# A mixture-of-experts stage on one Trainium2 core: VectorE's work around the first expert pair put in another order

## The chip, the cores and the metric

The kernel runs on one core of a Trainium2 chip. The time is device time in microseconds (us) of the whole program. The run with the profiler takes one execution apart; its span goes from the first to the last instruction.

## The reference

The program is two model blocks one behind the other, on 512 tokens of 1024 values in float32. The change touches the last stage of the second block, a mixture of 32 experts in 4 groups:

```python
def hier_moe(h, router_group_w, router_expert_w, w_gate, w_up, w_down):
    ...                                   # one group per token, two experts of 8 in it
    gate = group_prob * top_p / jnp.sum(top_p, axis=-1, keepdims=True)
    expert_id = (group_idx[:, None] * EXPERTS_PER_GROUP + top_local).astype(jnp.int32)
    ...                                   # tokens sorted by expert into slots
    def expert_block(args):
        xblk, e = args
        a = xblk @ w_gate[e]
        b = xblk @ w_up[e]
        return (jax.nn.silu(a) * b) @ w_down[e]
    yb = lax.map(expert_block, (xb, block_expert)).reshape(P, D)
    out = jnp.zeros((N + 1, D), jnp.float32).at[slot_tok].add(yb.astype(jnp.float32) * slot_gate[:, None])
    return out[:N].astype(h.dtype)
```

An expert's weights are three matrices of 1024 x 512 values (gate, up and down).

## The kernel before, in words

Each expert has 56 slots for tokens; what does not fit is handled by a loop at the very end (`overflow`), for which `spill` works out the tables. Experts go in pairs (16 of them, `blks`), and four pairs, an octet, share one gather.

`route` finds for each token its two experts and their slot numbers (`dest`). `build_S` turns `dest` into one-hots `S3` for the 448 slots of an octet, with 16 operations on VectorE (lines 1663 and 1664), and up to two that shift `dest` (`db`, line 1654). `gather_T` multiplies the tokens by these one-hots: 64 matmuls, out of which VectorE and ScalarE write the gathered tokens `hT` (`mhT`). `slot_rows` lays the slot numbers (`rows`) and gates (`grow`) of all tokens along the free dimension. From them, for each pair, `slots` makes the one-hots `ST` that later bring the results back to the tokens, and `gates` sums up the gate of each slot (`us`; line 1749, four operations and a sum, line 1753).

The products of a pair: `gate_up` multiplies `hT` by gate and up weights of one expert (two halves of the weights, four transfers of 1 MB, 32 matmul instructions), and `gu_out` on ScalarE scales the result by `us` (line 1804). `act_T` transposes it on TensorE and makes `h2`: tanh on ScalarE (line 1821) and two products on VectorE (lines 1822 and 1823). `down` multiplies by the down weights. `y_out` splits the output in two parts for the sums (ScalarE line 1862, VectorE line 1863), and `combine` adds it to the tokens: 16 matmuls with `ST`, and eight additions on VectorE (line 1872).

The loop of `moe` (lines 1454 on) goes over the pairs p: the first expert's gate and up product of p, the down product of the second expert of p-1, the transposes, the second expert's product with the sums of p-1 and the slots of p between its two halves, the gather where p ends an octet, the gates of p+1, the down product of the first expert of p, the transposes of the second.

What sets the order: TensorE's instructions run in the order of the source (`self.ordered(nc.tensor)`). On the other engines a scheduler puts the instructions in an order of its own; a call of `self.after(a, b)` makes it put a behind b without a wait on the chip. Each engine then works its queue off in that order, so that a waiting instruction holds up what stands behind it. Tiles have tags with a number of buffers; the scratch of `route` and `spill` has the tags yh0 and yl0, which `y_out` uses afterwards. The tile `h2` has the tag "rt" in the pool `rp` with one buffer (line 522), "hx" in the first pair and "S3" at the very end. Weights go through 16 buffers of 1 MB, loaded from SyncE's queue in the order of use.

Of the kernel before, what the change touches and what calls it, by code (L numbers as in the profile page):

```python
# [10 lines left out]
F32 = mybir.dt.float32  # L11
# [6 lines left out]
ALU = mybir.AluOpType  # L18
# [111 lines left out]
class Model:  # L130
# [1289 lines left out]
    def moe(self, psd):  # L1420
# [9 lines left out]
        blks = []  # L1430
# [8 lines left out]
        nb = NPAIR  # L1439
# [10 lines left out]
        self.slot_rows()  # L1450
        blks[0]["first"] = True
        ov = []
        for p in range(nb):
            more = p + 1 < nb

            def sums():
                if p:
                    self.combine(blks[p - 1], [(t, n) for n in range(2) for t in range(NT)])
                self.slots(blks[p])
                if more and p % 4 == 3:  # L1460
                    self.build_S(octs[p // 4 + 1])

            self.gate_up(blks[p], 0, not p, None if more else sums)
            if not p:
                self.gates(blks[0])
                self.gu_out(blks[0], 0)
            elif more:
                self.down(blks[p - 1], 1)
                self.act_T(blks[p], 0)
                self.y_out(blks[p - 1])  # L1470
            self.gate_up(blks[p], 1, half=sums if more else lambda: self.act_T(blks[p], 0))
            if more:
                if not p:
                    self.act_T(blks[0], 0, "hx")
                if p % 4 == 3:
                    self.gather_T(octs[p // 4 + 1])
                self.gates(blks[p + 1])
                self.down(blks[p], 0)
                self.act_T(blks[p], 1, "rt" if p else "hx")
                if not p:  # L1480
                    ov.extend(self.spill(mc))
                if p + 2 == nb:
                    self.down(blks[p], 1)
                    self.y_out(blks[p])
            else:
                self.down(blks[p], 0, lambda: self.act_T(blks[p], 1, "S3"))
# [115 lines left out]

    def spill(self, mc):

# [13 lines left out]
        ones = sc[:, 3 * NE:4 * NE]  # L1618
        V.memset(ones, 1.0)
        V.tensor_tensor_scan(end, ones, nb, initial=0.0, op0=ALU.mult, op1=ALU.add)  # L1620
# [22 lines left out]

    def build_S(self, blk):

# [5 lines left out]
        for h in range(blk["n"] // n):  # L1651
            if h or not isinstance(blk["base"], float) or blk["base"]:
                db = wk.tile([P, 2 * NT], F32, tag=f"db{h}", name="db")
                V.tensor_scalar(out=db, in0=dest, scalar1=blk["base"] + h * n if h else blk["base"], scalar2=None,
                                op0=ALU.subtract)
                ds.append(db)
            else:
                ds.append(dest)
# [61 lines left out]

    def slots(self, blk):

        wk, V = self.wk, self.nc.vector
        blk["ST"] = [wk.tile([P, S], F32R, tag=f"ST{s}", name=f"ST{s}") for s in range(2)]
        for s, o in enumerate(blk["ST"]):
            c = self.pcol[:, s, blk["pair"]:blk["pair"] + 1]
            V.tensor_scalar(out=o, in0=self.rows[:, 0, :], scalar1=c, scalar2=None, op0=ALU.is_equal)
            V.scalar_tensor_tensor(out=o, in0=self.rows[:, 1, :], scalar=c, in1=o.bitcast(F32), op0=ALU.is_equal,
                                   op1=ALU.add)

# [10 lines left out]

    def gates(self, blk):

        wk, V = self.wk, self.nc.vector
        a = wk.tile([P, 2, 2], F32, tag="ga", bufs=2, name="ga")
        for j in range(2):
            for i in range(2):
                junk = wk.tile([P, S], BF16, tag="gj", name="gj")
                V.scalar_tensor_tensor(out=junk, in0=self.rows[:, i, :], scalar=self.ucol[:, j, blk["pair"]:blk["pair"] + 1],  # L1749
                                       in1=self.grow[:, i, :], op0=ALU.is_equal, op1=ALU.mult,  # L1750
                                       accum_out=a[:, i, j:j + 1])
        us = wk.tile([P, 2], F32, tag="us", bufs=2, name="us")
        V.tensor_tensor(us, a[:, 0, :], a[:, 1, :], op=ALU.add)
        blk["us"] = us
# [22 lines left out]

    def gate_up(self, blk, j, hold=False, half=None):
        nc, wk = self.nc, self.wk
# [16 lines left out]
        blk["pg", j] = pg  # L1796
        if not hold:
            self.gu_out(blk, j)

# [12 lines left out]
    def act_T(self, blk, j, tag="rt"):  # L1812
# [9 lines left out]
        V.scalar_tensor_tensor(out=th, in0=th, scalar=1.0, in1=pv[:, :, 0, :], op0=ALU.add, op1=ALU.mult)  # L1822
        V.scalar_tensor_tensor(out=th, in0=th, scalar=0.5, in1=pv[:, :, 1, :], op0=ALU.mult, op1=ALU.mult)  # L1823
        blk["h2", j] = th
# [42 lines left out]
    def combine(self, blk, parts):  # L1867
        for t, nh in parts:
            ps = self.att()
            self.combine_mm(blk, t, nh, ps)  # L1870
            xv = self.x[:, t, nh * 512:(nh + 1) * 512]
            self.nc.vector.tensor_tensor(xv, ps, xv, op=ALU.add)  # L1872

# [130 lines left out]
```

## Time and profile before

| | us |
|---|---|
| median of 3 runs | 1753.62 |
| lowest, highest run | 1750.8, 1754.26 |
| the profiled execution | 1755.62 |
| its span | 1753.8 |

In the span TensorE's matmuls are busy for 97%, its weight loads 71% (beside the matmuls), VectorE 58%, ScalarE 34% and GpSimd 5%. The mixture of experts takes the last 500 us or so of the span. Times in a view of the profile are counted from the start of the span; a row names the engine, the source line, the tile that is written and the ones that are read. A bracket behind a row is the idle time of that engine ahead of it, and whose work ended it.

### The profile page before, as it was taken

To read this page: it belongs to the slowest core of one execution; us is meant where nothing else is said; L and a number is where in the kernel's file an instruction comes from. 1 tells how busy PE (TensorE), PEld (TensorE's weight loads), DVE (VectorE), ACT (ScalarE), POOL (GpSimd) and SP (SyncE) were. 2 spreads that over 40 slices of the span, in tenths; PEclk is the share of its full clock that TensorE was granted. 3 is DMA by queue.
4 is the path that set the end of the run, shared out by engine and by line. 5 is a ranking of instruction groups with operands and counts; after the bars stand their busy time and mean duration, and the time that the engine had idled before them with its cause. 6 is when DMAs were issued, how large, how long until landed. Compare 5 with 4: busy or idle time off the path is not lost.

```text
span 1753.8 us, 24034 instructions
## 1 busy us (share of the span) xinstructions
PE 1708.9 (97%) x9122; PEld 1238.9 (71%) x9122; DVE 1012.4 (58%) x2523; ACT 595.8 (34%) x1219; POOL 91.5 (5%) x130
## 2 busy tenths in 40 slices
PE   8999999999999999999999999999999999999996
PEld 7888888878878888888878777778833534445333
DVE  7655463663756555454566888774584555454334
ACT  7643333432545332232346534433301111111112
POOL 0000000000000110110002000000200000000001
PEclk9999999999999999999999999999999999999998
DMA  8633233223223223222422342327399999999993
GB/s 255 184 97 89 80 85 96 84 85 91 66 92 97 73 86 106 86 73 73 111 61 55 104 100 74 93 65 305 127 384 420 414 419 420 419 420 420 419 420 123
DMA packets 199561, 318.75 MB, mean 182 GB/s; under 512 B 18949, under 2 KB 160006, under 8 KB 174738
## 3 DMA queue, kind: packets, MB, share of 16 engines
q1 hardware_dynamic: 199442, 317.17, 50.9%
q8 instruction: 73, 1.20, 0.3%
q14 instruction: 46, 0.38, 0.1%
HBM read 312.13 MB, written 5.01 MB: 181 GB/s over the span
## 4 chain that ended last, share of the span: by engine, by line
PE 88%; DVE 6%; ACT 2%; DMA 1%; issue 1%; POOL 0%; SPq 0%; POOLq 0%; ACTq 0%; DVEq 0%
PE acc L149 50%; PE pg L236 12%; PE att L149 7%; PE att L236 7%; PE pd L236 6%; PE trp L154 3%; PE trp L236 1%; DVE wl L211 1%; PE trp L149 1%; DVE gj L1749 1%; DVE cy L1201 0%; ACT wh L210 0%; DMA kvf<-kvd 0%; PE att L154 0%; ACT hH L249 0%
## 5 line engine op out<-in xcount | busy, mean ns | idle before, releaser
L211 DVE TENSOR_TENSOR wl<-raw,wh 128x1024 fp32r<-128x1024 f32 x184 | 225.6, 1227 | 191.5 <-ACT wh L210 183.1
L149 PE MATMUL acc<-hL,wh 128*128 128x512 f32 (+1 forms) x760 | 298.2, 393 | 0.0
L149 PE MATMUL acc<-hH,wl 128*128 128x512 f32 (+1 forms) x760 | 297.6, 392 | 0.0
L149 PE MATMUL acc<-hH,wh 128*128 128x512 f32 (+1 forms) x760 | 296.1, 390 | 0.1
L210 ACT ACTIVATE wh<-raw 128x1024 fp32r<-128x1024 f32 x184 | 194.6, 1060 | 269.5 <-PE acc L149 253.2
L236 PE MATMUL pg<-mw,mhT 128*64 128x512 f32 x1024 | 229.8, 596 | 0.0
L236 PEld LDWEIGHTS pg<-mw,mhT 128*64 128x64 f32 x1024 | 69.5, 137 | 130.8 <-issue 128.2
L149 PEld LDWEIGHTS acc<-hL,wh 128*128 128x128 f32 x760 | 143.2, 188 | 25.3
L149 PEld LDWEIGHTS acc<-hH,wl 128*128 128x128 f32 x760 | 143.2, 188 | 25.1 <-issue 1.0
L149 PEld LDWEIGHTS acc<-hH,wh 128*128 128x128 f32 x760 | 143.0, 189 | 24.9 <-ACT hH L249 0.3
L149 PE MATMUL acc<-wh,hL 128*128 128x256 f32 (+1 forms) x384 | 129.4, 338 | 0.4 <-DVE hL L253 0.4
L149 PE MATMUL acc<-wh,hH 128*128 128x256 f32 (+1 forms) x384 | 129.2, 337 | 0.3 <-ACT hH L249 0.3
L149 PE MATMUL acc<-wl,hH 128*128 128x256 f32 (+1 forms) x384 | 129.2, 336 | 0.0
L149 PE MATMUL acc<-wh,oh 128*128 128x512 f32 x320 | 126.8, 396 | 1.4 <-ACT oh L249 1.4
L149 PE MATMUL acc<-wl,oh 128*128 128x512 f32 x320 | 125.9, 394 | 0.0
L149 PE MATMUL acc<-wh,ol 128*128 128x512 f32 x320 | 125.9, 394 | 0.0
L236 PE MATMUL pd<-mw,h 128*64 128x512 f32 (+1 forms) x544 | 117.5, 574 | 4.7 <-DVE h L1823 4.7
L1804 ACT ACTIVATE gu<-pg,us 128x512 f32<-128x512 f32 x32 | 22.0, 687 | 265.7 <-PE pg L236 265.7
L1863 DVE TENSOR_TENSOR yl<-pd,yh 128x512 fp32r<-128x512 f32 x30 | 19.3, 686 | 132.3 <-ACT yh L1862 132.3
L236 PEld LDWEIGHTS pd<-mw,h 128*64 128x64 f32 x544 | 38.7, 138 | 76.1 <-issue 67.1
L1872 DVE TENSOR_TENSOR x<-att,x 128x512 f32<-128x512 f32 x120 | 73.1, 682 | 31.6 <-PE att L236 31.6
L149 PEld LDWEIGHTS acc<-wh,hH 128*128 128x128 f32 x384 | 72.9, 190 | 8.5 <-ACT hH L249 1.0
(563 smaller groups left out, 2783.3 us busy)
## 6 DMA issues: line engine op xcount, KB each, us to landing
mw<-in_w_gate_dram SPq DMA_DIRECT2D x64, 1024.0 KB
mw<-in_w_up_dram SPq DMA_DIRECT2D x64, 1024.0 KB
mw<-in_w_down_dram SPq DMA_DIRECT2D x62, 1024.0 KB
raw<-in_fox_w_in_dram SPq DMA_DIRECT2D x56, 512.0 KB
raw<-in_w_out_dram SPq DMA_DIRECT2D x40, 512.0 KB
raw<-in_w_in_dram SPq DMA_DIRECT2D x28, 512.0 KB
raw<-in_ret_w_in_dram SPq DMA_DIRECT2D x20, 512.0 KB
raw<-in_w_mem_kv_dram SPq DMA_DIRECT2D x16, 512.0 KB
```

Source lines behind the costliest of these rows:

```text
L149: self.pe.matmul(o, l, r, start=start, stop=stop)
L154: self.pe.transpose(o, i, self.ident[b:b + n, b:b + n])
L210: nc.scalar.activation(h, raw, AF.Copy)
L211: nc.vector.tensor_tensor(l, raw, h.bitcast(F32), op=ALU.subtract)
L236: ins = getattr(eng, name)(*a, **k)
L1749: V.scalar_tensor_tensor(out=junk, in0=self.rows[:, i, :], scalar=self.ucol[:, j, blk["pair"]:blk["pair"] + 1], in1=self.grow[:, i, :], op ...
L1804: nc.scalar.activation(gu, pg.rearrange("p (n k) -> p k n", k=4), AF.Copy, scale=blk["us"][:, j:j + 1])
L1863: V.tensor_tensor(l, pd, h.bitcast(F32), op=ALU.subtract)
L1872: self.nc.vector.tensor_tensor(xv, ps, xv, op=ALU.add)
```

## The change

The order of some of the work is changed; no operation is added or taken away.

- `gates` of pair 0 comes ahead of the first product in the source, and the scaling of that product needs no special case.
- In pair 0 the transposes of the first expert, and then the slots, come between the two halves of the second expert's product; before, the slots were there, and the transposes behind the product.
- `slots`, `gates` (but for pair 0), the one-hots of later octets (through `db`) and the memset in `spill` are ordered behind the latest of a chosen set of VectorE operations, `self.last`: the last product of `h2`, the last addition of the sums, the last slot or gate operation, whichever came last in the source.
- The one-hots of the next octet are made behind the sums of the third pair of an octet, not the fourth.
- The gates of pair p+1 come behind the down product and the transposes of pair p.
- In the last pair but one the transposes of the second expert come between the halves of the first expert's down product.

```diff
         self.slot_rows()
         blks[0]["first"] = True
+        self.gates(blks[0])
...
-                self.slots(blks[p])
-                if more and p % 4 == 3:
-                    self.build_S(octs[p // 4 + 1])
-
-            self.gate_up(blks[p], 0, not p, None if more else sums)
-            if not p:
-                self.gates(blks[0])
-                self.gu_out(blks[0], 0)
-            elif more:
+                self.slots(blks[p], self.last)
+                if p + 2 < nb and p % 4 == 2:
+                    self.build_S(octs[p // 4 + 1], self.last)
+
+            def first():
+                self.act_T(blks[0], 0, "hx")
+                sums()
+
+            self.gate_up(blks[p], 0, None if more else sums)
+            if p and more:
                 self.down(blks[p - 1], 1)
                 self.act_T(blks[p], 0)
                 self.y_out(blks[p - 1])
-            self.gate_up(blks[p], 1, half=sums if more else lambda: self.act_T(blks[p], 0))
+            self.gate_up(blks[p], 1, (sums if p else first) if more else lambda: self.act_T(blks[p], 0))
             if more:
-                if not p:
-                    self.act_T(blks[0], 0, "hx")
                 if p % 4 == 3:
                     self.gather_T(octs[p // 4 + 1])
-                self.gates(blks[p + 1])
-                self.down(blks[p], 0)
-                self.act_T(blks[p], 1, "rt" if p else "hx")
+                self.down(blks[p], 0, (lambda: self.act_T(blks[p], 1)) if p + 2 == nb else None)
+                if p + 2 < nb:
+                    self.act_T(blks[p], 1, "rt" if p else "hx")
+                self.gates(blks[p + 1], self.last)
                 if not p:
-                    ov.extend(self.spill(mc))
+                    ov.extend(self.spill(mc, self.last))
...
-        V.memset(ones, 1.0)
+        self.after(V.memset(ones, 1.0), last)
...
-    def build_S(self, blk):
+    def build_S(self, blk, last=None):
...
-                V.tensor_scalar(out=db, in0=dest, scalar1=blk["base"] + h * n if h else blk["base"], scalar2=None,
-                                op0=ALU.subtract)
+                i = V.tensor_scalar(out=db, in0=dest, scalar1=blk["base"] + h * n if h else blk["base"], scalar2=None,
+                                    op0=ALU.subtract)
+                if last:
+                    self.after(i, last)
...
-    def slots(self, blk):
+    def slots(self, blk, last):
...
-            V.tensor_scalar(out=o, in0=self.rows[:, 0, :], scalar1=c, scalar2=None, op0=ALU.is_equal)
-            V.scalar_tensor_tensor(out=o, in0=self.rows[:, 1, :], scalar=c, in1=o.bitcast(F32), op0=ALU.is_equal,
-                                   op1=ALU.add)
+            i = V.tensor_scalar(out=o, in0=self.rows[:, 0, :], scalar1=c, scalar2=None, op0=ALU.is_equal)
+            self.after(i, last)
+            self.last = V.scalar_tensor_tensor(out=o, in0=self.rows[:, 1, :], scalar=c, in1=o.bitcast(F32),
+                                               op0=ALU.is_equal, op1=ALU.add)
...
-    def gates(self, blk):
+    def gates(self, blk, last=None):
...
+                if last:
+                    self.after(x, last)
...
-        V.tensor_tensor(us, a[:, 0, :], a[:, 1, :], op=ALU.add)
+        self.last = V.tensor_tensor(us, a[:, 0, :], a[:, 1, :], op=ALU.add)
...
-        V.scalar_tensor_tensor(out=th, in0=th, scalar=0.5, in1=pv[:, :, 1, :], op0=ALU.mult, op1=ALU.mult)
+        self.last = V.scalar_tensor_tensor(out=th, in0=th, scalar=0.5, in1=pv[:, :, 1, :], op0=ALU.mult, op1=ALU.mult)
...
-            self.nc.vector.tensor_tensor(xv, ps, xv, op=ALU.add)
+            self.last = self.nc.vector.tensor_tensor(xv, ps, xv, op=ALU.add)
```

## Rows read from the trace of the kernel before

**Rows 1.** Busy time by stretch: length, busy us per engine, clock share, DMA share, GB/s.

```profile
1247.20:1250.50 3.30, 0.02 (x1) 0.00 (x0) 1.43 (x7) 1.80 (x10) 0.00 (x0) 0.89 0.00 0
1250.50:1256.60 6.10, 6.04 (x16) 5.42 (x17) 3.96 (x16) 0.00 (x0) 1.56 (x9) 0.50 0.00 1
...
1284.60:1287.90 3.30, 0.02 (x1) 0.00 (x0) 3.30 (x12) 0.50 (x2) 0.00 (x0) 0.91 1.02 422
1287.90:1290.70 2.80, 2.79 (x8) 0.94 (x10) 2.20 (x8) 0.00 (x0) 0.00 (x0) 0.50 1.01 418
...
1320.00:1700.70 380.70, 380.70 (x1752) 169.25 (x1748) 178.63 (x373) 48.03 (x90) 0.00 (x0) 1.00 1.01 419
1700.70:1702.10 1.40, 0.03 (x1) 0.00 (x0) 0.84 (x2) 0.38 (x1) 0.00 (x0) 1.00 1.00 415
...
1716.00:1724.20 8.20, 8.20 (x41) 2.77 (x39) 1.73 (x4) 1.07 (x2) 0.00 (x0) 1.00 0.28 103
```

**Rows 2.** Timeline of VectorE ahead of the gather: start, duration, operation, idle before.

```profile
1246.06 0.42 DVE L1562 TENSOR_REDUCE dest<-sc 128x8 f32<-128x256 f32 x1
1249.07 0.09 DVE L1619 MEMSET sc<- 128x32 f32 x1 [2.59 <-ACT sc L1584]
1249.07 0.13 DVE L1654 TENSOR_SCALAR db<-dest 128x8 f32<-128x8 f32 x1
```

**Rows 3.** Timeline of TensorE from the first gather to the first down product.

```profile
1250.56 0.71 PE L236 MATMUL att<-S,xH 128*128 128x448 f32 x1 [3.34 <-DVE S L1664]
...
1266.46 1.95 PE L236 MATMUL att<-ident,dest 128*128 128x128 f32 x16
...
1270.13 13.90 PE L236 MATMUL pg<-mw,mhT 128*64 128x512 f32 x64
1283.97 0.66 PE L236 MATMUL trp<-ident,gu 128*128 128x128 f32 x4
1287.91 5.03 PE L236 MATMUL pd<-mw,h 128*64 128x512 f32 x16 [3.29 <-DVE h L1823]
```

**Rows 4.** Timeline of ScalarE and VectorE in pair 0.

```profile
1277.29 0.69 ACT L1804 ACTIVATE gu<-pg,us 128x512 f32<-128x512 f32 x1 [6.35 <-PE pg L236]
...
1285.76 0.75 DVE L1749 SCALAR_TENSOR_TENSOR gj<-rows,pcol,grow 128x512 bf16<-128x512 uint16 x1
...
1287.44 0.42 DVE L1823 SCALAR_TENSOR_TENSOR h<-h,trp 128x256 f32<-128x256 f32 x1
```

**Rows 5.** Timeline of TensorE in the last pair but one.

```profile
1702.11 3.65 PE L236 MATMUL pd<-mw,h 128*64 128x512 f32 x16 [1.38 <-DVE h L1823]
```

**Rows 6.** The chain that ended last, in order of time: start, duration, work.

```profile
1293.62 7.02 PE pg L236 x32
...
1308.24 3.98 PE att L236 x16
...
1315.80 3.43 PE pd L236 x16
1319.82 7.02 PE pg L236 x32
...
1368.20 13.28 PE att L236 x64
```

**Rows 7.** Timeline of VectorE: the first operation of `spill`, and the split behind it.

```profile
1293.66 0.19 DVE L1612 COPY sc<-att 128x32 f32<-128x32 f32 x1 [3.52 <-PE att L236]
...
1304.76 1.29 DVE L1863 TENSOR_TENSOR yl<-pd,yh 128x512 fp32r<-128x512 f32 x2 [2.58 <-ACT yh L1862]
```

**Rows 8.** Timeline of VectorE, ScalarE and TensorE in a steady pair.

```profile
1340.73 1.41 DVE L1728 SCALAR_TENSOR_TENSOR ST<-rows,pcol,ST 128x512 fp32r<-128x512 uint16 x2
...
1346.93 0.42 DVE L1823 SCALAR_TENSOR_TENSOR h<-h,trp 128x256 f32<-128x256 f32 x1
...
1353.18 0.69 ACT L1804 ACTIVATE gu<-pg,us 128x512 f32<-128x512 f32 x1 [6.73 <-PE pg L236]
...
1356.41 0.66 PE L236 MATMUL trp<-ident,gu 128*128 128x128 f32 x4
```

More of the change, by code (lines that the diff above doesn't have):

```diff
@@ L1601, in route, with spill @@
             G.tensor_tensor(self.gr[:, :, i, 1:2], gx[:, :, 2 * i:2 * i + 1], r, op=ALU.mult)
-    def spill(self, mc):
+    def spill(self, mc, last):
         nc = self.nc
@@ L1748, in gates @@
                 junk = wk.tile([P, S], BF16, tag="gj", name="gj")
-                V.scalar_tensor_tensor(out=junk, in0=self.rows[:, i, :], scalar=self.ucol[:, j, blk["pair"]:blk["pair"] + 1],
-                                       in1=self.grow[:, i, :], op0=ALU.is_equal, op1=ALU.mult,
-                                       accum_out=a[:, i, j:j + 1])
+                x = V.scalar_tensor_tensor(out=junk, in0=self.rows[:, i, :], scalar=self.ucol[:, j, blk["pair"]:blk["pair"] + 1],
+                                           in1=self.grow[:, i, :], op0=ALU.is_equal, op1=ALU.mult,
+                                           accum_out=a[:, i, j:j + 1])
+                if last:
+                    self.after(x, last)
         us = wk.tile([P, 2], F32, tag="us", bufs=2, name="us")
-        V.tensor_tensor(us, a[:, 0, :], a[:, 1, :], op=ALU.add)
+        self.last = V.tensor_tensor(us, a[:, 0, :], a[:, 1, :], op=ALU.add)
         blk["us"] = us
@@ L1776, in gates_any, with gate_up @@
         blk["us"] = us
-    def gate_up(self, blk, j, hold=False, half=None):
+    def gate_up(self, blk, j, half=None):
         nc, wk = self.nc, self.wk
@@ L1796, in gate_up @@
         blk["pg", j] = pg
-        if not hold:
-            self.gu_out(blk, j)
+        self.gu_out(blk, j)
     def gu_out(self, blk, j):
```

## The prediction

> **What bounds the kernel now.** I read the busy share and the granted clock by stretch first [rows 1]. Over 380.70 us of the experts' stage the matmul engine is busy for all 380.70 us, at a clock share of 1.00. The weights' transfers take a DMA share of 1.01 beside it, and VectorE works less than half of the time (178.63 us). So in that stage TensorE is the bound. A re-ordering of VectorE's work can pay only where TensorE stands still, or runs at a low clock.
>
> The same view shows where that is. From 1247.2 to 1250.5 us and from 1284.6 to 1287.9 us PE is busy for 0.02 us of 3.30 us. After each of these two holes comes a stretch with a clock share of 0.50, the lower one of the two levels (1.2 of 2.4 GHz): 6.10 us and 2.80 us. Near the end there is a third hole, 1.40 us long, through which the clock stays at 1.00. A wide hole is therefore paid twice, as idle time and as slow matmuls behind it.
>
> Next I read who ends each hole. In the timeline of VectorE [rows 2] the position of the tokens (`dest`, line 1562) is done at 1246.06 + 0.42 = 1246.48 us. The first operation that builds the one-hots for the gather (`db`, line 1654) needs nothing else, yet it starts at 1249.07. Ahead of it in VectorE's queue stands a memset of 32 columns, line 1619, which belongs to `spill`, work that is wanted much later. It writes into a scratch that ScalarE's exponentials (line 1584) still read, and its row says so: 2.59 us idle, released by that line. The gather on TensorE follows the first one-hots [rows 3]: it starts at 1250.56.
>
> The second hole [rows 3, 4]: the transposes of the first expert's product start at 1283.97, but the second of VectorE's two products for `h2` (line 1823) starts at 1287.44 only, 3.5 us later, because gates of later pairs (line 1749, 0.75 us each) stand in front of it and between the two. The down product waits 3.29 us for that line and starts at 1287.91.
>
> The third hole [rows 5]: the down product of the last pair but one waits 1.38 us for `h2`, directly behind its transposes, with no foreign work between.
>
> **The change, part by part.**
>
> *The memset of `spill` is put behind the gates of pair 1.* VectorE can start `db` at 1246.48 plus a few hundredths, say 1246.51. From `db` to the gather's start takes 1250.56 - 1249.07 = 1.49 us [rows 2, 3], so the gather starts near 1248.00, 2.56 us earlier. The hole, now 3.3 us, shrinks to 1248.00 - 1247.2 = 0.8 us. Those 1.49 us hold the one-hots of one of four token tiles; a tile's eight matmuls for half of the columns take 13.28 / 8 = 1.66 us at the full clock [rows 6], so VectorE stays ahead of TensorE.
>
> The clock: holes of 3.3 us were followed by the low level, the hole of 1.40 us was not [rows 1]. At 0.8 us I take it that the clock stays up. The first gather took 1266.46 - 1250.56 = 15.90 us [rows 3], a later one of the same 64 matmuls 13.28 us [rows 6]: 2.62 us less. Bounds of this part: 2.56 us (the clock falls all the same) to 5.18 us; I take 5.18, as 0.8 us is far nearer to 1.40 than to 3.3.
>
> The Trainium skill (TensorE: Matmul & The Clock Gate, section "Part 1: The HAM clock gate") says that the moment at which the clock's level is decided runs free of the program, so that one and the same kernel meets it at another place in each run. By that rule a hole of this size is no sure thing in either direction, and this part would be worth 2.56 us in some executions; no run here shows that so far.
>
> *Gates of pair 0 ahead of the first product, `h2` of expert 0 inside the second product, everything else on VectorE behind it.* The gates of pair 0 hide where they did: ScalarE scales the first product at 1277.29 [rows 4], directly behind its end (1270.13 + 13.90 / 2 = 1277.08, [rows 3]). The transposes of expert 0 move between the two halves of the second product, near 1280.6, so `h2` has the second half, 3.4 us, to become ready. From the transposes' start to the down product it needs what the third hole shows where nothing foreign stands in the queue: the transposes, 0.66 us [rows 3], and 1.38 us behind them [rows 5], 2.0 us in all. The slots of pair 0, the gates of pair 1, the one-hots of the next four pairs and the memset are all ordered behind some `h2` or sum, so they can't get in front of it. The down product then starts when the products and the transposes are through, 1283.97 + 0.6 = 1284.6, which takes out 3.29 us. And without the hole there is no low clock: from the down product to the next product it took 1293.62 - 1287.91 = 5.71 us, in a later pair 1319.82 - 1315.80 = 4.02 us [rows 3, 6], to which four small matmuls of `spill` add about 0.1 us here: 1.6 us less. Sum of this part 4.9 us; bounds 3.3 us (clock) to 4.9 us.
>
> *What comes late instead.* VectorE's work of this stretch moves back: `h2` of expert 1 (0.9 us), gates of pair 1 (4 x 0.83 = 3.3 us, [rows 4]), then `spill`, which took 1304.76 - 2.58 - 1293.66 = 8.5 us with one `h2` inside [rows 7]. In times of the trace before, less the 4.9 us, the transposes of expert 1 end near 1288.6, so this is done near 1301.5; the split of pair 0's output, which reuses `spill`'s scratch and feeds the sums, is wanted when the sums start, 1308.24 - 4.9 = 1303.3 [rows 6], and costs 1.29 us, the first half of it 0.65 us [rows 7]. It just fits, so I cost it at nothing; if it doesn't, up to 1.5 us comes back.
>
> *The one-hots of the next four pairs behind the third pair's sums.* Now at most 4 x 1.49 = 6.0 us of VectorE work stand ahead of `h2` and gates in three pairs. In a steady pair VectorE ends its slots at 1340.73 + 1.41 = 1342.14, and the second product of `h2` starts at 1346.93, the first some 0.45 us before it [rows 8]; so `h2` slips by 1342.14 + 6.0 - 1346.48 = 1.7 us at most. Its down product starts a whole gate and up product (7.02 us, [rows 6]) after the transposes. Cost nothing.
>
> *Gates behind `h2` in each pair.* In a steady pair `h2` is done at 1346.93 + 0.42 = 1347.35; four gates add 3.3 us, so they are done by 1350.8, and ScalarE wants them at 1353.18 [rows 8]. Covered by 2.4 us; cost nothing. In the three pairs with one-hots 0.7 us of this are left, if `h2` slips by the 1.7 us.
>
> *The last pair but one.* The transposes for expert 1 move between the halves of its down product. But `h2` has the tag "rt" in a pool of one buffer (line 522), and the second half of the down product still reads the old tile. So the tanh must wait for the product's end all the same, and the 1.38 us [rows 5] stay. Bounds 0 to 1.4 us gained; I take 0.
>
> *DMA.* Nothing is added to a queue. SyncE's weight loads start when the first product frees its buffers, and that moves with the gather, by 5.2 us. From there on the stream is full (419 GB/s, share 1.01). After 1716 us it thins out to a share of 0.28, and ends before the last products' weights are used at 1724.2 [rows 1]: TensorE runs some 8 us behind it. The 4.9 us of the second part eat into this cover and leave about 3 us or more.
>
> Sum: 5.18 + 4.9 = 10.1 us. The profiled run took 1755.62 us (span 1753.8 us and 1.8 us around it), so it would be 1745.5 us. It lies 2.0 us above the median of the runs, 1753.62 us; against that median I forecast **1743.6 us**, 0.57% less.
>
> **Rivals.** *A. The clock falls in front of the gather all the same.* For it: the hole does not go away. Against it: the clock share was 1.00 through the 1.40 us hole [rows 1]. Time 1743.6 + 2.6 = 1746.2 us. The rule of the Trainium skill above is this rival's; the trace speaks against it so far. *B. `spill` runs into the sums of pair 0* (above): up to 1.5 us back, 1745.1 us. *C. The change doesn't do what it says at the gather*: another operation waits in VectorE's queue in the memset's place, or the one-hots wait for something that the memset's wait hid. Against it: `db` and the memset start at the same 1249.07, and `dest`, the only input, was there 2.59 us earlier [rows 2]. The 5.2 us stay: 1748.8 us. *D. The last hole closes too*: 1743.6 - 1.4 = 1742.2 us.
>
> *E. Slower.* The gates now come behind `h2` in all pairs. The point from which this decides: done later than about 1355.7, in the times of the steady pair, since then the scaling (0.69 us) ends after 1356.41, when TensorE wants to transpose [rows 8]. Should the queue's order put them behind the split of the previous pair's output too, which comes after 1356.41, then 1.29 + 3.3 + 0.69 = 5.3 us lie between that time and the transposes; in each of 14 pairs that is 74 us, about 1818 us. Against it: the source issues the gates ahead of that split.
>
> **How the numbers follow.** Forecast 0.70, A 0.08, B 0.07, C 0.05, D 0.04, E 0.03, and 0.03 for gains here that an unseen stall gives back. The runs of before lie between 2.8 us below and 0.6 us above their median, and the two bounds above reach 2.6 us up and 1.4 us down; so 1741.0 to 1747.0 us holds the forecast, A, B and D, and leaves out C and E. A measurement of this kernel can tell some 0.2%, 3.5 us, from no change. Faster by more than that: forecast, A, B, D and C (4.8 us), 0.93 with a little off for C. Within: 0.03. Slower: 0.04.
>
> **What would show it.** Right: `db` near 1246.5 us with no memset ahead of it; the gather starts near 1248.0 and takes 13.3 us at clock share 1.00; no hole between transposes and down product in pair 0; gate and up product of pair 1 starts 10 us earlier than before, and all later products keep that distance; the last hole is still there. Wrong: a stretch at 0.50 behind 1248 us (A); idle PE at the sums of pair 0 (B); idle PE once a pair in front of the transposes (E). The prediction falls if products in the steady pairs no longer follow each other without idle time, or if weights come late at the end.

## The result, and the profile after

| | before | after |
|---|---|---|
| median of 5 runs, us | 1754.26 | 1744.64 |
| lowest, highest, us | 1750.8, 1755.47 | 1744.25, 1746.32 |
| the profiled execution, us | 1755.62 | 1744.48 |
| its span, us | 1753.8 | 1742.7 |

The changed kernel takes 0.9947 of the time before, with a 95% interval of 0.9935 to 0.9958. The forecast was 1743.6 us with a range of 1741.0 to 1747.0.

I read the profile after in the order of the prediction. First busy time by stretch, columns as in [rows 1]:

```profile
1243.70:1247.00 3.30, 2.51 (x24) 2.32 (x23) 2.95 (x10) 2.40 (x12) 1.77 (x10) 1.00 0.27 114
1247.00:1260.30 13.30, 13.28 (x64) 12.13 (x65) 5.79 (x17) 3.09 (x10) 1.57 (x9) 1.00 0.00 1
...
1278.50:1282.00 3.50, 3.50 (x19) 0.98 (x15) 0.06 (x1) 0.69 (x1) 0.00 (x0) 1.00 1.01 419
...
1297.30:1682.00 384.70, 384.70 (x1772) 172.60 (x1772) 195.34 (x424) 48.21 (x90) 0.00 (x0) 1.00 1.01 420
1682.00:1694.20 12.20, 10.81 (x52) 3.54 (x50) 7.48 (x18) 1.07 (x2) 0.00 (x0) 1.00 1.02 422
```

The clock column says 1.00 in every line. The stretches at 0.50 of [rows 1] are gone, and so are the two holes of 3.3 us. In the 384.70 us from the first sums on TensorE still has no idle time. Holes are left in the first line, ahead of the gather, and in the last.

VectorE ahead of the gather (start, duration, operation), to be laid beside [rows 2]:

```profile
1245.05 0.42 DVE L1563 TENSOR_REDUCE dest<-sc 128x8 f32<-128x256 f32 x1
1245.50 0.17 DVE L1655 TENSOR_SCALAR db<-dest 128x8 f32<-128x8 f32 x1
...
1287.19 0.09 DVE L1620 MEMSET sc<- 128x32 f32 x1
```

`dest` is done at 1245.47, and `db` starts 0.03 us later with no idle time ahead of it. The memset now runs 42 us behind `db`, after the gates of pair 1.

TensorE from the first gather to pair 1, and the last pair but one, beside [rows 3, 5]; the bracket is the idle time ahead and its releaser:

```profile
1247.02 0.44 PE L236 MATMUL att<-S,xH 128*128 128x448 f32 x1 [0.82 <-DVE S L1667]
...
1260.32 1.95 PE L236 MATMUL att<-ident,dest 128*128 128x128 f32 x16
1263.99 10.47 PE L236 MATMUL pg<-mw,mhT 128*64 128x512 f32 x48
1274.39 0.66 PE L236 MATMUL trp<-ident,gu 128*128 128x128 f32 x4
1274.98 3.65 PE L236 MATMUL pg<-mw,mhT 128*64 128x512 f32 x16
1278.46 3.60 PE L236 MATMUL pd<-mw,h 128*64 128x512 f32 x16
...
1282.67 7.09 PE L236 MATMUL pg<-mw,mhT 128*64 128x512 f32 x32
...
1690.96 3.23 PE L236 MATMUL pd<-mw,h 128*64 128x512 f32 x14 [1.39 <-DVE h L1828]
```

The gather waits 0.82 us where it waited 3.34, and its 64 matmuls take 1260.32 - 1247.02 = 13.30 us. The transposes lie between the halves of the second product, and the first down product has no bracket: it follows at once. The hole near the end is as it was.

Two more places where the prediction saw little cover (the time by which work may come late before TensorE waits for it). The first three lines are the end of `spill`, the split of pair 0's output and TensorE's first matmul of the sums. The other two are the gates' sum made in the turn p = 2 of the loop, the first that builds one-hots, and the scaling that uses it:

```profile
1293.52 0.17 DVE L1631 CAST tab<-ebt 1x18 int32<-1x18 f32 x1
1293.89 1.29 DVE L1868 TENSOR_TENSOR yl<-pd,yh 128x512 fp32r<-128x512 f32 x2 [0.20 <-ACT yh L1867]
...
1297.30 0.50 PE L236 MATMUL att<-yh,ST 128*128 128x512 f32 x1
...
1340.21 0.16 DVE L1759 TENSOR_TENSOR us<-ga 128x2 f32<-128x2 f32 x1
...
1342.28 0.69 ACT L1809 ACTIVATE gu<-pg,us 128x512 f32<-128x512 f32 x1 [6.72 <-PE pg L236]
```

The split is done at 1295.18, and the sums start at 1297.30 with no bracket, that is, without a wait. The gates are there 1.91 us before ScalarE scales, and ScalarE's bracket names the product, not the gates.

### The profile page after: what moved, and what is told of

It reads as the page before. It is cut to its first block, busy times and chain, and to the rows that moved or that the text cites. A ratio compares the mean times of both kernels' runs of the same rounds, so it can differ in the third digit from the quotient of the medians.

```text
span 1742.7 us, 24020 instructions
## 1 busy us (share of the span) xinstructions
PE 1704.7 (98%) x9122; PEld 1236.6 (71%) x9122; DVE 1012.9 (58%) x2523; ACT 596.6 (34%) x1219; POOL 91.6 (5%) x130
## 4 chain that ended last, share of the span: by engine, by line
PE 89%; DVE 5%; ACT 2%; DMA 2%; issue 1%; SPq 0%; POOL 0%; POOLq 0%; ACTq 0%; DVEq 0%
PE acc L149 50%; PE pg L236 13%; PE att L149 8%; PE att L236 7%; PE pd L236 6%; PE trp L154 3%; PE trp L236 1%; DVE wl L211 1%; PE trp L149 1%; DMA raw<-in_w_mem_kv_dram 1%; DVE cy L1201 0%; ACT wh L210 0%; PE att L154 0%; ACT hH L249 0%; DMA kvf<-kvd 0%
## 5 line engine op out<-in xcount | busy, mean ns | idle before, releaser
L149 PEld LDWEIGHTS acc<-wh,hL 128*128 128x128 f32 x384 | 72.9, 190 | 8.0 <-DVE hL L253 0.7
```

What stands on the lines that cost most here:

```text
L149: self.pe.matmul(o, l, r, start=start, stop=stop)
```

## The experiments

The table gives, for each kernel, four lengths of its trace in us, worked out from starts of rows: from the end of `dest` to the first gather's start; from there to the matmuls of `slot_rows` (the gather's length); from the start of the first product to that of pair 1; from the end of `dest` to the end of the span. The last column is how long the granted clock stood at 0.50 in this stage, at which hole.

| kernel | to gather | gather | product 0 to 1 | to the end | half clock |
|---|---|---|---|---|---|
| before | 4.08 | 15.90 | 23.42 | 507.35 | 6.8 (first), 3.4 (second) |
| after | 1.56 | 13.30 | 18.68 | 497.22 | none |
| e1_memset_only | 1.56 | 13.15 | 23.74 | 502.41 | 3.4 (second) |
| e2_rest_only | 4.08 | 13.29 | 18.68 | 500.17 | none |
| e3_move_only | 4.08 | 14.50 | 18.68 | 501.22 | 3.4 (first) |
| e4_order_only | 1.56 | 13.15 | 20.20 | 499.02 | none |
| e5_changed_again | 1.56 | 13.15 | 18.68 | 497.22 | none |
| e6_second_h2_buffer | 1.56 | 13.15 | 18.68 | 495.74 | none |
| e7_transposes_back | 1.56 | 13.15 | 18.68 | 497.20 | none |
| e8_fewer_warmups | 1.56 | 14.71 | 18.68 | 498.92 | 3.4 (first) |
| e9_more_warmups | 6.31 | 13.30 | 23.73 | 507.30 | 3.4 (second) |
| e10_three_times_gates | 1.56 | 13.16 | 18.68 | 528.89 | 3 x 3.4 (later pairs) |

Times and ratios below are against runs of the kernel before on the same chip: medians 1754.06 us beside e1 to e4, 1755.09 beside e5 to e8, 1755.71 beside e9 and e10.

**The memset alone.** The kernel before, with the memset of `spill` ordered behind the last product of `h2` that stands ahead of it in the source, and nothing else.

```diff
-        V.memset(ones, 1.0)
+        self.after(V.memset(ones, 1.0), last)
...
-        V.scalar_tensor_tensor(out=th, in0=th, scalar=0.5, in1=pv[:, :, 1, :], op0=ALU.mult, op1=ALU.mult)
+        self.hl = V.scalar_tensor_tensor(out=th, in0=th, scalar=0.5, in1=pv[:, :, 1, :], op0=ALU.mult, op1=ALU.mult)
...
-                    ov.extend(self.spill(mc))
+                    ov.extend(self.spill(mc, self.hl))
```

> The kernel before with one edit: the memset of spill is ordered behind the second product of h2 of pair 0's second expert. On every engine but VectorE the order stays, and on VectorE only the memset moves. Theory: the first hole is the memset's wait on ScalarE and the half clock behind it, worth 2.56 + 2.62 = 5.2 us; the second hole stays as it is. So 5.2 us less than before, the gather starts at the full clock 0.8 us after the last warm-up matmul. Rival A (the clock falls at 0.8 us of idle time all the same): 2.6 us less. Rival C (something else holds the one-hots up): no difference.

Measured: 1750.67 us, ratio 0.9975 (0.9965 to 0.9986). Two windows of its trace, and the down product of pair 0:

```profile
1247.70:1260.90 13.20, 13.16 (x65) 12.10 (x66) 5.93 (x19) 3.12 (x10) 1.56 (x9) 1.00 0.01 2
...
1282.40:1285.80 3.40, 3.40 (x10) 1.02 (x12) 2.14 (x8) 0.00 (x0) 0.00 (x0) 0.59 1.02 422
```

```profile
1282.35 1.33 PE L236 MATMUL pd<-mw,h 128*64 128x512 f32 x4 [3.29 <-DVE h L1823]
```

The gather starts 1.56 us behind `dest` and runs at full clock; the second hole, 3.29 us, and the low clock behind it are untouched. So the memset was the cause of 2.52 us of the first hole (rival C falls; 0.82 us stay), and the two holes can be dealt with one at a time. From `dest` to the end the trace is 4.94 us shorter. The medians differ by 3.4 us, the ratio's interval means 2.5 to 6.1 us.

**The rest alone.** The changed kernel with the memset free again.

```diff
-        self.after(V.memset(ones, 1.0), last)
+        V.memset(ones, 1.0)
```

> The changed kernel with the memset of spill free again; on VectorE it then stands ahead of the first one-hots as before, and nothing else differs in the order. Theory: only the second hole closes, 3.3 us idle and 1.6 us of half clock, so 4.9 us less than before; with e1 it sums up to the whole change (10.1 us). Rival (the two parts overlap, or one hides the other's gain): the sum of both comes out clearly larger or smaller than the change.

Measured: 1749.82 us, ratio 0.998 (0.9968 to 0.9992). From the first product to pair 1 its trace takes 18.68 instead of 23.42 us, 4.74 less; the medians differ by 4.2 us. At the gather stood a surprise; the start of the gather, and the window behind it:

```profile
1249.43 0.44 PE L236 MATMUL att<-S,xH 128*128 128x448 f32 x1 [3.34 <-DVE S L1667]
```

```profile
1250.10:1256.90 6.80, 6.80 (x34) 6.19 (x34) 4.41 (x14) 1.27 (x2) 1.56 (x9) 1.00 0.00 0
```

The hole of 3.34 us is the one of [rows 3], to the hundredth. Here no low clock follows it, where the kernel before paid 6.8 us of it. So this trace is 7.2 us shorter from `dest` to the end, and not only by the 4.74. It is also the fastest of the twelve runs; three of them lie at 1755.9 to 1756.5 us, and what they paid was not traced.

Do e1 and e2 sum up to the whole change? By the ratios they give 0.25 + 0.20 = 0.45%, beside 0.53% for the change: no difference within the intervals. In the traces the two places don't touch each other: 1.56 us to the gather and 18.68 us from product 0 to 1 are the same alone and together.

**Only the move of the transposes.** The kernel before; the transposes of expert 0 go between the halves of the second product, with no order on VectorE.

```diff
+            def first():
+                self.act_T(blks[0], 0, "hx")
+                sums()
+
...
-            self.gate_up(blks[p], 1, half=sums if more else lambda: self.act_T(blks[p], 0))
+            self.gate_up(blks[p], 1, half=(sums if p else first) if more else lambda: self.act_T(blks[p], 0))
             if more:
-                if not p:
-                    self.act_T(blks[0], 0, "hx")
```

> The kernel before with one edit: the transposes of expert 0 (act_T) between the halves of the second expert's product. The order of VectorE's queue around h2 stays as in before, with gates of later pairs and one-hots ahead of it. Theory: what makes the second hole is the place of h2 in VectorE's queue, which is busy without a pause from the slot rows on, so h2 comes hardly earlier: 0 to 0.4 us less than before. Rival: the place of the transposes on TensorE makes it; then 3.3 to 4.9 us less.

Measured: 1749.31 us, ratio 0.9969 (0.9957 to 0.9981). I was wrong: the second hole closes. VectorE in pair 0 of the kernel before, then VectorE and TensorE in this one:

```profile
1267.75 0.68 DVE L1711 TENSOR_SCALAR rows<-att 128x512 uint16<-128x512 f32 x1
...
1286.43 0.42 DVE L1822 SCALAR_TENSOR_TENSOR h<-h,trp 128x256 f32<-128x256 f32 x1
```

```profile
1266.13 0.68 DVE L1713 TENSOR_SCALAR rows<-att 128x512 uint16<-128x512 f32 x1
...
1280.84 0.41 DVE L1824 SCALAR_TENSOR_TENSOR h<-h,trp 128x256 f32<-128x256 f32 x1
...
1281.84 0.41 DVE L1825 SCALAR_TENSOR_TENSOR h<-h,trp 128x256 f32<-128x256 f32 x1
```

```profile
1278.91 0.66 PE L236 MATMUL trp<-ident,gu 128*128 128x128 f32 x4
...
1282.98 3.60 PE L236 MATMUL pd<-mw,h 128*64 128x512 f32 x16
```

`h2` is done at 1282.25, and the product, at 1282.98, waits for nothing. VectorE works without a gap from `rows` to `h2` in both, so the place of `h2` in its queue can be read off the time: 14.7 us behind the first row of `rows` here, 18.7 us in the kernel before. In the whole view 12 gate operations stand ahead of it here, 16 in the kernel before. I had taken the queue for fixed. But the scheduler chooses VectorE's order, and where the transposes come earlier in the source it sets `h2` ahead of some of the gates. There is 0.7 us to spare; nothing in the source holds it so.

At the gather this trace has the hole of 3.34 us once more, and this time 3.4 us of half clock behind it:

```profile
1250.30:1253.70 3.40, 3.36 (x10) 3.06 (x11) 3.40 (x12) 0.00 (x0) 0.00 (x0) 0.56 0.00 0
```

From `dest` to the end the trace is 507.35 - 501.22 = 6.1 us shorter. Of this 4.74 us are the second hole, and 1.4 us the shorter half clock at the first, which the edit does not touch.

**Only the order.** The changed kernel with the transposes back behind the second product.

```diff
...
-            self.gate_up(blks[p], 1, (sums if p else first) if more else lambda: self.act_T(blks[p], 0))
+            self.gate_up(blks[p], 1, sums if more else lambda: self.act_T(blks[p], 0))
             if more:
+                if not p:
+                    self.act_T(blks[0], 0, "hx")
```

The slots of pair 0, which came behind that `h2`, are ordered behind the gates of pair 0 in it.

> The changed kernel with the transposes of expert 0 back behind the second expert's product (the slots of pair 0 ordered behind the first gates); all the order on VectorE is the change's. Theory: with nothing foreign ahead of h2, the second hole is as wide as the last one in before, 1.4 us, the clock stays up through it, and the change loses just that: 10.1 - 1.4 = 8.7 us less than before. Rival: the order on VectorE alone closes the hole (10.1 us less); or the clock falls at 1.4 us here (about 7 us less).

Measured: 1747.34 us, ratio 0.9954 (0.994 to 0.9969).

```profile
1277.91 0.65 PE L236 MATMUL trp<-ident,gu 128*128 128x128 f32 x4
1280.00 3.65 PE L236 MATMUL pd<-mw,h 128*64 128x512 f32 x16 [1.44 <-DVE h L1827]
```

```profile
1280.00:1283.60 3.60, 3.60 (x17) 1.07 (x17) 0.00 (x0) 0.00 (x0) 0.00 (x0) 1.00 0.99 412
```

With nothing foreign in VectorE's queue, it takes 1280.00 - 1277.91 = 2.09 us from the start of the transposes to the product behind `h2`; the prediction had put 2.0 together out of [rows 3, 5]. The hole shrinks to 1.44 us, and the clock stays at 1.00 behind it. From `dest` to the end the trace is 8.33 us shorter; the medians differ by 6.7 us, with 5.4 to 10.5 us in the interval. The move is worth the other 20.20 - 18.68 = 1.52 us. So order and move do much of the same work: the order alone leaves 1.44 us of the second hole, the move alone (e3) none. What the order adds to the move is room. In e3 `h2` is done 0.7 us before its product starts; in the changed kernel it is done at 1276.44, 2.0 us before the product at 1278.46:

```profile
1276.02 0.42 DVE L1828 SCALAR_TENSOR_TENSOR h<-h,trp 128x256 f32<-128x256 f32 x1
```

**The changed kernel once more**, unchanged, beside e6 to e8.

> The changed kernel unaltered, to stand beside the next three on the same chip. Expected 9.4 us less than before, as already measured (1744.6 us), with no stretch at half clock in the experts' stage.

Measured: 1745.17 us, ratio 0.9947 (0.9927 to 0.9968).

**A second buffer for `h2`** in the last pair but one, so that its moved transposes need not wait for the tile.

```diff
-                self.down(blks[p], 0, (lambda: self.act_T(blks[p], 1)) if p + 2 == nb else None)
+                self.down(blks[p], 0, (lambda: self.act_T(blks[p], 1, "hx")) if p + 2 == nb else None)
```

> The changed kernel, with h2 of the second expert of the last pair but one in the tile of the first pair (tag hx), which is free by then; the order on all engines stays the same. Theory (the one buffer of tag rt holds the tanh back, whatever the place of the transposes): with a buffer of its own h2 is ready behind the first half of the down product, the last hole closes from 1.39 us to 0.3 us or less, 1.1 to 1.4 us less than the changed kernel. Rival (the hole is the latency from transposes to product and the buffer is not what it waits for): no difference.

Measured: 1745.37 us, ratio 0.995 (0.9931 to 0.9968), against 1745.17 us for the changed kernel. The tanh in the changed kernel first, then tanh and products in this one:

```profile
1689.62 0.38 ACT L1826 ACTIVATE h<-trp 128x256 f32<-128x256 f32 x1 [3.46 <-PE pd L236]
```

```profile
1691.05 0.38 ACT L1826 ACTIVATE h<-trp 128x256 f32<-128x256 f32 x1 [1.58 <-PE trp L236]
```

```profile
1690.36 0.66 PE L236 MATMUL trp<-ident,gu 128*128 128x128 f32 x4
1690.94 5.37 PE L236 MATMUL pd<-mw,h 128*64 128x512 f32 x24
```

The releaser changes from `pd`, which reads the one buffer, to `trp`, and the 1.39 us are gone: from `dest` to the end the trace is 497.22 - 495.74 = 1.48 us shorter. The medians don't show it; the runs of this kernel lie between 1742.98 and 1750.29 us.

**The transposes of the last pair but one back where they were.**

```diff
-                self.down(blks[p], 0, (lambda: self.act_T(blks[p], 1)) if p + 2 == nb else None)
-                if p + 2 < nb:
+                self.down(blks[p], 0)
+                if True:
```

> The changed kernel without its edit in the last pair but one: the transposes of the second expert stand behind the whole down product again. Theory: the edit brought nothing, since the tanh waited for the same buffer; hole of 1.4 us as before, no difference to the changed kernel (within 0.1 us in the trace). Rival: the edit is worth up to 1.4 us, then this one is slower by that.

Measured: 1745.66 us, ratio 0.9953 (0.9936 to 0.9971); from `dest` to the end 497.20 us. The hole has the same size as with the move:

```profile
1691.87 0.66 PE L236 MATMUL trp<-ident,gu 128*128 128x128 f32 x4
1693.90 3.65 PE L236 MATMUL pd<-mw,h 128*64 128x512 f32 x16 [1.38 <-DVE h L1828]
```

So this edit of the change brings nothing by itself.

**Fewer warm-up matmuls.** Ahead of the gather the kernel runs matmuls whose results nobody reads. With fewer of them the changed kernel has its old hole again, though VectorE is as early as in the change: a test of the clock by itself.

```diff
-NWARM = 28
+NWARM = 18
```

> The changed kernel with 18 warm-up matmuls in place of 28; those behind the token counts are gone, so TensorE stands still for some 3.1 us ahead of the gather, which starts when it did. Theory after e2 and e3 (a hole of 3.3 us was followed by 0, 3.4 or 6.8 us of half clock in three executions): the gather takes between 13.3 and 15.9 us, from execution to execution, so the median is 0 to 2.6 us above the changed kernel and the runs spread more than its 2 us. Rival (a hole of more than 3 us always costs both steps): 2.6 us slower in all runs; rival (the hole doesn't matter): no difference.

Measured: 1747.66 us, ratio 0.9956 (0.994 to 0.9971), 2.5 us above the changed kernel; all nine runs lie between 1746.4 and 1749.97 us. The gather's start, and the windows behind it:

```profile
1248.90 0.44 PE L236 MATMUL att<-S,xH 128*128 128x448 f32 x1 [3.14 <-DVE S L1667]
```

```profile
1248.90:1250.30 1.40, 1.40 (x7) 1.30 (x8) 1.40 (x6) 0.98 (x6) 0.00 (x0) 1.00 0.05 12
1250.30:1253.70 3.40, 3.40 (x11) 3.04 (x10) 2.40 (x9) 0.00 (x0) 0.65 (x4) 0.50 0.00 0
```

The gather starts 1.56 us behind `dest`, as in the change, and still takes 14.71 us instead of 13.15. The hole in front of it costs time on its own account, by the clock alone. One step of half clock, 3.4 us, followed here, so the rival that both steps always follow does not hold in this trace. The runs don't settle it: their median is at the 2.6 us of that rival, and they spread over 3.6 us, where those of the changed kernel beside them spread over 1.8. That the hole sometimes costs nothing is not seen in them; the lowest of the nine is above five of those six runs.

**More warm-up matmuls** in the kernel before, to fill its first hole without touching VectorE.

```diff
-NWARM = 28
+NWARM = 54
```

> The kernel before with 54 warm-up matmuls in place of 28, so that TensorE works on until about 1250 us, where the gather starts; nothing else changes. The idle time of the first hole shrinks from 3.34 us to under 0.5 us without any operation of VectorE being earlier: the gather starts when it did (4.1 us after dest). Theory: the start is set by the one-hots alone, and the half clock by the idle stretch; so no half clock in the gather (13.2 to 13.3 us in the profile), the second hole as before: 0 to 2.6 us less than before, by how often the clock fell there. Rival (the memset's effect was through the clock alone): as fast as e1, 4.4 us less.

Measured: 1756.75 us, ratio 1.0009 (0.9996 to 1.0022): no difference. The warm-up matmuls, the gather's start and the window of the gather:

```profile
1245.25 8.28 PE L149 MATMUL trp<-x,ident 128*128 128x128 f32 x72
1253.29 0.46 PE L236 MATMUL att<-S,xH 128*128 128x448 f32 x1
```

```profile
1253.30:1266.60 13.30, 13.30 (x68) 12.12 (x67) 3.68 (x12) 2.13 (x4) 1.56 (x9) 1.00 0.01 2
```

I had sized this badly. Each of the 26 is two matmul instructions here, and 72 of them take 8.28 us, 0.115 each; they run on past the moment when the one-hots are ready. The gather starts 6.31 - 4.08 = 2.23 us later, runs at full clock (13.30 us, 2.60 less than in the trace before), and next to nothing is left: the second hole costs 0.31 us more in this trace, and from `dest` to the end it is 507.30 us beside 507.35. So the run fills the hole, but it does not leave the gather's start alone, as it was meant to; what a filling of the right length would give was not tested. This one gave back in waiting what it won by the clock.

**Gates three times.** The changed kernel with eight more gate operations into a scratch, ahead of the four real ones of each pair but the first, in the same order. It brings rival E about: gates that come late.

```diff
+        if last:
+            a2 = wk.tile([P, 2, 2], F32, tag="ga2", bufs=2, name="ga2")
+            for k in range(8):
+                i, j = k % 2, k // 2 % 2
+                ...                       # the same operation into a2
+                self.after(x, last)
+            last = x
```

> The changed kernel with the four gate operations of each pair but pair 0 done three times (two of the three into a scratch that nobody reads), each time behind h2: 8 x 0.8 = 6.4 us more on VectorE in each pair, between h2 and the sum of the gates. In the changed kernel the sum of the gates ends 5.8 us behind the start of the transposes, the scaling needs 0.7 us, and the next transposes come at 11.0 us. Theory (cover of 4.5 us until TensorE waits): 6.4 us exceed it by 1.9 to 2.0 us, in 13 pairs 25 us, and 3 to 6 us more in pair 0 and 1 with spill behind them: 26 to 34 us slower than the changed kernel. Rival (VectorE's time between the products is not covered): about 6.4 x 15 = 96 us slower; rival (the cover is wider): under 10 us.

Measured, in two runs: 1780.25 us, ratio 1.0144 (1.0125 to 1.0162). Beside 0.9947 that is 2.0% or some 35 us more than the changed kernel. One of the two is the traced execution, which has 13.7 us of half clock near 1028 us, ahead of this stage; so the stage is better read from the trace. From `dest` to the end it is 31.7 us longer, in the upper part of the 26 to 34 that I expected. What TensorE waited for (total us, times, longest), and four of its starts:

```profile
PE trp L236 <- ACT gu L1819: 20.8, 14, 2.0
```

```profile
1307.59 0.50 PE L236 MATMUL att<-yl,ST 128*128 128x512 f32 x1 [1.96 <-DVE yl L1878]
...
1360.56 0.66 PE L236 MATMUL trp<-ident,gu 128*128 128x128 f32 x4 [1.98 <-ACT gu L1819]
...
1485.15 0.65 PE L236 MATMUL trp<-ident,gu 128*128 128x128 f32 x4 [2.00 <-ACT gu L1819]
...
1611.56 0.65 PE L236 MATMUL trp<-ident,gu 128*128 128x128 f32 x4 [2.00 <-ACT gu L1819]
```

The first of these starts is the sums of pair 0, rival B's place: with the longer gates the split comes too late for them. The others are transposes. All 14 pairs get a hole in front of the transposes, where the prediction put E: 1.35 us in ten of them, 1.26 in pair 1, 1.98 to 2.00 in the three whose gates stand behind one-hots. Eight gates are 6.4 us of VectorE (0.80 each from start to start), so the pairs had 6.4 - 1.35 = 5.0 us of cover, and those three 4.4. I had expected 4.5 us of cover, holes of 1.9 to 2.0 us in 13 pairs, and priced no low clock: that the sum fits is partly luck. Behind three of the four holes of 1.96 to 2.00 us the clock fell as well; the stretch behind the first:

```profile
1308.70:1312.10 3.40, 3.40 (x10) 2.62 (x9) 3.04 (x6) 0.00 (x0) 0.00 (x0) 0.50 1.00 417
```

## Why the prediction was right

**The bound and the places.** That TensorE is the bound, and that re-ordered work on VectorE pays only at its holes, held throughout: everything behind pair 1 takes 460.01 us in the trace after, 460.28 before (the start of pair 1's product to the end of the span).

**The memset.** Predicted: 2.56 us for the start and 2.62 us for the clock. Measured: 4.08 - 1.56 = 2.52 us and 15.90 - 13.30 = 2.60 us. The wait had one cause, as the equal starts in [rows 2] said. The first term is firm: the start comes 1.56 us behind `dest` in e1 as in the change. The second is not a price but one draw: the same hole of 3.34 us cost the gather 15.90 - 13.29 = 2.6 us in the execution that I read, 14.50 - 13.29 = 1.2 us in e3 and nothing in e2. The size that I took for the rule was the upper end of the bounds that I had given, and the sentence beside the sum, that this part would be worth 2.56 us in some executions, is what e2 shows. Taken over runs, the memset's part is 0.25% by e1 against before and 0.33% by the changed kernel against e2, 4.4 and 5.8 us with intervals of some 2 us and more: around the 5.18 us, and no sharper.

**The second hole.** Predicted 4.9 us, measured 23.42 - 18.68 = 4.74 us: 3.29 us of hole, the rest the clock. The stated cause was right, gates of later pairs in front of `h2`; one-hots of the next octet (line 1664), which I did not name there, stood between them. The split between the two edits was not seen: I wrote that the order on VectorE keeps the gates away, and the move gives `h2` room; e3 and e4 show that the move alone makes the scheduler send `h2` ahead and closes the hole, and that the order alone leaves 1.44 us.

**What comes late instead.** Predicted: it just fits, 1.8 us between the end of `spill` and the sums, less 1.29 for the split, so 0.5 us. In the trace after, the split ends 1297.30 - 1295.18 = 2.12 us before the sums start, and `spill` 3.6 us before. Of the difference 0.9 us is my slip: `h2` of the second expert is the one inside the 8.5 us of `spill`, and I counted it twice. Rival B did not happen; e10 shows what it would have looked like.

**The gates.** The prediction had 4.9 us between the end of the gates (1350.8) and the point from which E decides (1355.7). By e10 it is 5.0 us in a plain pair and 4.4 behind one-hots, where 4.9 - 1.7 = 3.2 were expected. In the turn p = 2 `us` is 1.91 us early, where I left 0.7. That `h2` slips by 1.7 us was an upper bound: from the transposes to `h2` it takes 1.76 us in that turn and 1.11 in the one before, a slip of 0.65.

**The last pair but one.** Predicted 0 with the reason that the pool has one buffer; measured 1.39 us for 1.38, the releaser of the tanh names the product that reads the tile, and e6 removes the hole by a second buffer. Rival D is what the edit would have given with it.

**DMA.** No weight came late. Counted from the weights' packets in the trace, the least distance between a transfer's end and its use went from 11.9 to 7.2 us, by the 4.7 us of the second part. I had started from 8 us, read off the thinning of the stream, and so saw less cover than there was.

**The sum.** Predicted 10.1 us; from the end of `dest` to the end of the span it is 507.35 - 497.22 = 10.13 us. The three terms above make 2.52 + 2.60 + 4.74 = 9.86 of it; the other 0.27 us come behind the start of pair 1, where I predicted nothing. The spans differ by 11.1 us, since `dest` came 1.0 us earlier in the execution after. That is not the change: nothing ahead of it was touched, and over the traces of this study `dest` ends between 1245.35 and 1252.11 us. Rival A, a low clock in front of the gather all the same, is in none of the seven traces with a hole of 0.82 us.

Where the terms fit to a few hundredths, some of it is luck: the sum was made against one execution, in which the first hole was followed by more half clock than in any other trace, and which was slower (1755.62 us) than the five runs beside the result. The medians fell by 9.6 us (and 9.9 in e5's comparison).

## What to carry to other kernels

Look where the bound engine stands still, ask whose instruction ends the wait, and then what stood ahead of that instruction in its own queue: a small operation for much later work, put early by a scheduler and waiting for a scratch, held up the whole chain for 2.5 us. A shorter memset could have saved no more than its own 0.09 us; an ordering edge took the 2.5 us out. But look first what cover the work that you push back has (here 5 us for the gates), since past that point it costs in every turn of the loop. Don't take a scheduler's order on one engine for fixed when you move work on another: in e3 it changed, for the better by chance. A step that is moved earlier gains nothing as long as its output tile has one buffer that the work before it still reads.

## What the runs showed of the hardware

The price of a hole in TensorE's work is not fixed. One of 3.1 to 3.3 us was followed by 6.8 us at half clock (before, first hole), by 3.4 us (before, e1 and e9, second hole; e3 and e8, first hole), or by none (e2, first hole). In before, e2 and e3 it is the same hole of 3.34 us, with the same warm-ups ahead of it and the same 64 matmuls behind. Behind holes of 1.44 us and less no trace shows a fall in this stage. Holes of 1.96 to 2.00 us were followed by 3.4 us at half clock three times in e10 and not the fourth time. The Trainium skill (TensorE: Matmul & The Clock Gate, section "Part 1: The HAM clock gate") says that the moment at which the level is decided runs free of the program; e2, e3 and the kernel before agree with it, with 0, 3.4 and 6.8 us behind the same 3.34 us.

This goes together with the scatter of the runs: before, they lie between 1750.5 and 1763.0 us beside e5, the changed kernel's there between 1744.8 and 1746.6. That the first hole's clock makes all of that difference was not tested; half-clock stretches ahead of this stage (near 1028 us, 3.4 us long in e6 and e7 and 13.7 us in e10) show that other places add to it. What decides whether a hole is followed by the low clock stays open.
